# Encoder layer on one core: adaLN's second half behind the first tokens' turns, early gate weights in blocks of 256 columns, and the first gate pair's B22 product ahead of T1 and T4

## The chip, the core and the metric

The program runs on one core of one Trainium2 chip. Five engines work from queues of their own and meet only through semaphores: TensorE (PE, matrix products, with its weight loads shown as PEld), VectorE (DVE), ScalarE (ACT), GpSimd (POOL) and SyncE (SP, which here only issues DMA transfers). A queue is strictly in order: an instruction that waits holds up all that stands behind it. The metric is the time of one execution on the device in microseconds (us), the median of several runs; lower is better.

## What is computed

One layer of an encoder over 1280 tokens (1024 of a prompt and 256 of a sample) with 1024 channels, all in float32:

```python
mod = c @ w_ada + b_ada
shift, scale, gate = jnp.split(mod[:, None, :], 3, axis=-1)
h = rms_norm(x, norm_g) * (1.0 + scale) + shift
p = h @ w_in
cb, cc, cx, cz, q, k, v, o, mz, gpre, gmerge = split_combined(p)
...
g_conv, g_mlstm = jnp.split(jax.nn.sigmoid(gmerge), 2, axis=-1)
merged = g_conv * (y_conv @ w_proj_conv) + g_mlstm * (y_m @ w_proj_mlstm)
return x + gate * (merged @ w_out)
```

"adaLN" is the first line: the vector c (one for the prompt, one for the sample) times w_ada gives a shift and a scale for each channel. The change lies where h is made and where the first products with w_in begin, those of the 2048 merge-gate columns (gmerge).

## The kernel before

**Tiling.** h is held turned, channels on the partitions. It is cut in four blocks by channel half (1: channels 0 to 511, 2: 512 to 1023) and token half (1: tokens 0 to 639, 2: 640 to 1279): B11, B21 (second channels, first tokens), B12 (first channels, second tokens), B22. A pair of column blocks of w_in (128 columns each) against these four is done with seven products in place of eight (Strassen's scheme, class `Strassen`, lines 640 to 746): B11, B21, T2, T3, T1, T4 and B22, where T1 = B12 - B11, T2 = B22 - T1, T3 = T2 - B11 and T4 = B21 - T2 are sums of data blocks, and the weights of T2, T3, T1 and B22 are sums of weight blocks ("comb", made by VectorE in line 666). Each product has float32 precision by three terms: data and weights are both split in a rounded high part H and a rest L (ScalarE casts H in line 369, VectorE subtracts to get L in line 370; for weights ScalarE casts wh in line 317 and GpSimd subtracts to get wl in line 318), and wh·H + wh·L + wl·H are added up. One product is 24 matmuls of 128x320 (line 794): four slices of channels, and in each two with wh·H, two with wh·L, two with wl·H. Its result lies in one of three PSUM buffers ("acc") until VectorE adds it to what it belongs to (line 710).

**How the program begins** (`beginning`, from line 376). The ten token blocks of x are loaded and normalised, and turned by TensorE (`turn_x`, line 437); ScalarE (442) or VectorE (445) applies scale and shift as it takes the result out of PSUM. Scale and shift come from adaLN, eight loads of w_ada of 1 MB in two halves each (`load_wa`, `adaln(i)`, products in line 508): loads 0 to 3 give the values of channel half 1, loads 4 to 7 those of channel half 2. After the fourth and the eighth, VectorE copies the sum (515), TensorE turns it (519), and VectorE makes scale and shift (492 to 494). Tiles are shared: load 5 takes the place of load 2 (b10H), load 6 that of 3 (b10L), load 7 that of 4 (b11H), so each of them waits until the older one has been used.

**Early weights.** B11 and B21 are there before the others. So the B11 and B21 products of the first block of each of six gate pairs (class `Corner`) run first, six with B11 and six with B21; their weights come by `early_load(j, n)`, six loads of 512 KB, three for j = 0 (first channels) and three for j = 1. A loaded buffer ("raw") serves two corners. There are three such buffers in all. Then come the other five products of pair 0, of pair 1 and so on, from buffers of the same pool.

**The order of the work** is fixed when the program is built: `Board` (line 45 on) takes operations with assumed durations, the things that they read and write, and a due step, and lays them out per engine by a list plan, due steps first where more than one can begin at once. `op(..., after=...)` adds operations that must come before. On the chip the queues then run as laid out. Names for what follows: "pair 0" and "pair 1" are the first two gate pairs after the corners; their products run as T2, T3, T1, T4, B22 each.

Of the kernel before, what the change touches and what calls it, by code (L numbers as in the profile page):

```python
# [16 lines left out]
P = 128  # L17
# [23 lines left out]
class Board:  # L41
# [30 lines left out]
    def op(self, eng, us, f, r=(), w=(), after=(), low=False, slack=0.0):  # L72

        o = self.Op()
        o.eng, o.us, o.f, o.low, o.step, o.n, o.played, o.slack = eng, us, f, low, self.step, len(self.ops), False, slack
        o.before = set(after)
        for t in r:
            if t in self.writer:
                o.before.add(self.writer[t])
        for t in w:  # L80
            o.before.update(self.readers.get(t, ()))
            if t in self.writer:
                o.before.add(self.writer[t])
        for t in w:
            self.writer[t], self.readers[t] = o, []
        for t in r:
            if t not in w:
                self.readers.setdefault(t, []).append(o)
        o.before.discard(o)
        o.bufs = list(dict.fromkeys(b for t in (*r, *w) for b in (t if isinstance(t, tuple) else (t,)) if isinstance(b, self.Buf)))  # L90
        for b in o.bufs:
            b.users.append(o)
        self.ops.append(o)
        return o
# [87 lines left out]
def encoder_kernel(  # L182
# [7 lines left out]
    V, A, G, PE = nc.vector, nc.scalar, nc.gpsimd, nc.tensor  # L190
# [114 lines left out]
    def load(kb, dst, src, r, w, low=False):  # L305
        op("SP", kb, lambda: dma(dst(), src), r=r, w=w, low=low)
# [4 lines left out]
    def raw_tile():  # L311
        return buf(wp, [P, 4, 2 * P], F32, "raw", 3)
# [8 lines left out]
    raw_a = {}  # L321

    def early_load(j, n):

        raw_a[j, n] = raw_a[j, n + 2] = raw = raw_tile()
        for i in range(2):
            c = CGM + (n + 2 * i) * P
            load(256, lambda i=i: raw[:, :, i * P:(i + 1) * P], win[:, 4 * j:4 * j + 4, c:c + P], (), [(raw, i)])


    xt = {jl: [buf(xp, [P, TH2], F32, "xt", 17, xp.tile([P, TH2], F32, tag="xt", name="xt")) for _ in range(4)]
# [46 lines left out]
    def beginning():  # L378
# [48 lines left out]
        def turn_x(cs, kts):  # L427

            t0, tn = cs[0] * P, len(cs) * P
            l, smp = t0 // TH2, int(cs[0] > 7)  # L430
            for kt in kts:
                px = misc_buf()
                dst, d0 = xt[kt // 4, l][kt % 4], t0 % TH2

                def turn(px=px, kt=kt):
                    for j, c in enumerate(cs):
                        PE.transpose(px[:, j * P:(j + 1) * P], x_at[c][0]()[:, kt * P:(kt + 1) * P], ident[:])

                op("PE", .14 * len(cs), turn, r=[x_at[c][1] for c in cs], w=[px])
                sc, sh, tok = s1[:, kt, smp:smp + 1], shf[:, kt, smp:smp + 1], ("s1", kt // 4)  # L440
                if kt % 2 == (cs[0] in (3, 8)):
                    op("ACT", .37 + .1 * len(cs), lambda px=px, dst=dst, d0=d0, sc=sc, sh=sh: A.activation(
                        dst[:, d0:d0 + tn], px[:, :tn], AF.Identity, bias=sh, scale=sc), r=[px, tok], w=[(dst, int(d0 > 0))])
                else:
                    op("DVE", .39 + .1 * len(cs), lambda px=px, dst=dst, d0=d0, sc=sc, sh=sh: V.tensor_scalar(
                        out=dst[:, d0:d0 + tn], in0=px[:, :tn], scalar1=sc, scalar2=sh, op0=ALU.mult, op1=ALU.add),
                       r=[px, tok], w=[(dst, int(d0 > 0))])
# [8 lines left out]
        def later_rows(first):  # L456
# [22 lines left out]

            op("DVE", .5, take, r=[pr], w=["cwh"])  # L480
            op("POOL", .2, lambda: G.memset(ones[:], 1.0), r=[pr], w=[("rows", r) for r in (RSH, RNG, RMH, RCW, RCB)])
        pada = {}
        sel = const.tile([P, 2, 2], F32, name="sel")
        half = (lambda i: ident[:, 64 * i:64 * i + 64].rearrange("p (j r) -> p j r", r=32)[:, :, 0:2])
        op("DVE", .15, lambda: V.tensor_tensor(out=sel[:], in0=half(0), in1=half(1), op=ALU.add), w=["sel"])
# [10 lines left out]
        def adaln(i):  # L496

            hf = i // 4
            if i == 0:
                pada[0] = buf(psX, [P, 2, 512], F32, "acc", 3)  # L500
            t = pada[0]
            for n, (wa, tok) in enumerate(wa_at[i]):
                kt = 2 * (i % 4) + n

                def mm(n=n, kt=kt, wa=wa):
                    for j in range(2):
                        g = 32 * (2 * n + j)
                        PE.matmul(t[g:g + 32, hf, :], cz4()[:, kt, :], wa()[:, j * 512:(j + 1) * 512],
                                  start=i % 4 == 0, stop=i % 4 == 3, tile_position=(0, g))

                op("PE", 1.1, mm, r=[ctok, tok], w=[(t, hf)])
            if i % 4 < 3:
                return
            pm, m = misc_buf(), buf(cp, [P, 4, P], F32, "comb", 5)
            op("DVE", .65, lambda: V.tensor_copy(m[:].rearrange("p a b -> p (a b)"), t[:, hf, :]), r=[(t, hf)], w=[m])

            def turn_mod():
                for r in range(4):
                    PE.matmul(pm[:, 4 * r:4 * r + 4], m[:, r, :], sel[:].rearrange("p j s -> p (j s)"), start=True, stop=True)

            op("PE", .9, turn_mod, r=[m, "sel"], w=[pm])
            op("DVE", .6, lambda: modulation(hf, pm), r=[pm, "cols"], w=[("s1", hf)])
# [92 lines left out]
    class Slice:  # L615


        def __init__(self, b, sl):
            self.b, self.sl, self.tok = b, sl, (b, sl.start)
# [16 lines left out]
    class Strassen:  # L636

        def __init__(self, ca, cb, o11, o21, o12, o22, pre=None):  # L640
            self.cols, self.o, self.p1 = (ca, cb), (o11, o21, o12, o22), pre
            jobs = [(self.w_11, "b11", self.e_11), (self.w_12, "b21", self.e_12), (self.w_t2, "t2", self.e_t2),
                    (self.w_t3, "t3", self.e_t3), (self.w_t1, "t1", self.e_t1), (self.w_22, "t4", self.e_t4),
                    (self.w_b22, "b22", self.e_b22)]
            self.jobs, self.away = jobs if pre is None else jobs[2:], None

        def load(self):
# [90 lines left out]
        def e_t1(self, acc):  # L738
            self.out(3, acc, self.u3)
            self.plus(acc, self.u2, self.u2)  # L740

        def e_t4(self, acc):
            self.out(1, acc, self.u3, True)

# [12 lines left out]
    class Corner:  # L757
# [7 lines left out]
            self.st.e_11(acc)  # L765

        def prep(self, j):
            raw, i = raw_a[j, self.n], self.n // 2 % 2
            return split_op(lambda: raw[:, :, i * P:(i + 1) * P], [(raw, i)])

    todo, made, at = [], {}, [0]
# [42 lines left out]
            store(320, th_dr[r * P:(r + 1) * P, sl], t, [t.tok])  # L814
        return f

    def gate_pair(n, pre=None):

        return Strassen(CGM + n * P, CGM + (n + 1) * P,
                        (None, save(n, lo_)), (None, save(n + 1, lo_)),  # L820
                        (None, save(n, hi_)), (None, save(n + 1, hi_)), pre)

    def og_pair(n):

# [411 lines left out]
        store(256, ex_dr[i], lambda: place[:, 0:4 * P], [place])  # L1236


    sts = {n: gate_pair(n, max(n // 2 - 2, 0)) for n in range(0, 12, 2)}
    corners = {n: Corner(n, sts[n]) for n in sts}  # L1240
    for j in range(2):
        for n in (8, 10, 0, 2, 4, 6):
            add(corners[n], [j])
    for n in range(0, 16, 2):
        add(sts.get(n) or gate_pair(n))
    for st in head_pairs(range(1)):
        add(st)
    ends = [len(todo)]
# [655 lines left out]
```

## Time and profile before

| | |
|---|---|
| time, median of 3 runs | 1684.71 us (1683.56 to 1684.81) |
| the profiled execution | 1683.56 us, of which the span of its instructions 1681.4 us |
| TensorE busy | 1637.1 us, 97% of the span |
| VectorE, ScalarE, GpSimd busy | 59%, 34%, 40% |
| TensorE's waits of over 3 us in the first 130 us | 4.7 us (for c), 3.3 us (for a w_ada load), 3.5 us (for VectorE, line 370) |
| DMA | 240.82 MB, mean 143 GB/s; 351 GB/s in the first 42 us |

A line of a timeline gives start, duration, engine, line of the kernel, operation, destination and sources, and in brackets how long the engine was idle before it and what ended that. Rows of a stretch of the span ("windows") give its length, the busy time of each engine with the number of instructions, the granted TensorE clock (PEclk, 1.00 is full), the DMA engines' share and the rate. "T1" below is a product that reads tiles named xt, as T4 does; B22 reads b11H and b11L, T2 reads t2H and t2L, T3 reads t3H and t3L.

### The profile page before, as it was taken

To read this page: it belongs to the slowest core of one execution; us is meant where nothing else is said; L and a number is where in the kernel's file an instruction comes from. 1 tells how busy PE (TensorE), PEld (TensorE's weight loads), DVE (VectorE), ACT (ScalarE), POOL (GpSimd) and SP (SyncE) were. 2 spreads that over 40 slices of the span, in tenths; PEclk is the share of its full clock that TensorE was granted. 3 is DMA by queue.
4 is the path that set the end of the run, shared out by engine and by line. 5 is a ranking of instruction groups with operands and counts; after the bars stand their busy time and mean duration, and the time that the engine had idled before them with its cause. 6 is when DMAs were issued, how large, how long until landed. Compare 5 with 4: busy or idle time off the path is not lost.

```text
span 1681.4 us, 27662 instructions
## 1 busy us (share of the span) xinstructions
PE 1637.1 (97%) x10528; PEld 1563.3 (93%) x10528; DVE 992.3 (59%) x1691; ACT 573.3 (34%) x1115; POOL 680.2 (40%) x499
## 2 busy tenths in 40 slices
PE   6999999999999999999999999999999999899997
PEld 2999999999999999999999999999888899898985
DVE  5785334555555566566666876651257677555655
ACT  3643332134553222222222212212256665333322
POOL 1233333335664666667666633333210102323412
PEclk8999999999999999999999999999999999999999
DMA  9334335324553122222122556458778855773631
GB/s 351 111 126 133 103 99 123 77 72 124 144 154 103 51 71 69 82 82 70 54 66 82 143 132 141 118 132 278 258 242 293 270 180 170 237 266 107 245 105 63
DMA packets 281528, 240.82 MB, mean 143 GB/s; under 512 B 96068, under 2 KB 236596, under 8 KB 281396
## 3 DMA queue, kind: packets, MB, share of 16 engines
q1 hardware_dynamic: 281364, 239.05, 47.1%
q8 instruction: 83, 1.36, 0.3%
q14 instruction: 49, 0.40, 0.1%
q10 hardware_dynamic: 32, 0.01, 0.0%
HBM read 170.12 MB, written 68.89 MB: 142 GB/s over the span
## 4 chain that ended last, share of the span: by engine, by line
PE 91%; DMA 4%; DVE 3%; ACT 1%; SPq 1%; issue 1%; DVEq 0%; ACTq 0%
PE acc L794 63%; PE u L1423 3%; PE qc L1383 3%; PE accd L1578 2%; PE accd L1579 2%; PE accd L1580 2%; PE accd L1792 2%; PE accd L1791 2%; PE accd L1790 2%; PE acc L1646 2%; PE acc L1647 2%; PE acc L1645 2%; PE misc L1506 1%; DMA b11H<-in_w_ada_dram 1%; PE misc L1466 1%; DVE xt L375 1%
## 5 line engine op out<-in xcount | busy, mean ns | idle before, releaser
L318 POOL TENSOR_TENSOR wl<-comb,wh 128x512 fp32r<-128x512 f32 x176 | 249.9, 1420 | 288.2 <-ACT wh L317 279.5
L710 DVE TENSOR_TENSOR q<-acc,q 128x640 f32<-128x640 f32 x272 | 220.9, 819 | 222.1 <-PE acc L794 219.8
L318 POOL TENSOR_TENSOR wl<-raw,wh 128x512 fp32r<-128x512 f32 x136 | 190.2, 1399 | 225.0 <-ACT wh L317 208.1
L794 PE MATMUL acc<-xt,wh 128*128 128x320 f32 x1408 | 265.3, 310 | 3.5 <-DVE xt L370 3.5
L794 PEld LDWEIGHTS acc<-xt,wh 128*128 128x128 f32 x1408 | 221.9, 189 | 4.0 <-DVE xt L370 3.8
L317 ACT CAST wh<-comb 128x512 fp32r<-128x512 f32 x176 | 108.8, 619 | 292.7 <-PE acc L794 268.8
L317 ACT CAST wh<-raw 128x512 fp32r<-128x512 f32 x136 | 84.3, 620 | 271.3 <-PE acc L794 213.2
L794 PE MATMUL acc<-xt,wl 128*128 128x320 f32 x704 | 161.0, 310 | 0.0
L1606 POOL TENSOR_TENSOR wl<-raw,wh 128x512 fp32r<-128x512 f32 x28 | 36.7, 1313 | 225.5 <-ACT wh L1605 219.2
L794 PEld LDWEIGHTS acc<-xt,wl 128*128 128x128 f32 x704 | 118.2, 189 | 0.0
L666 DVE TENSOR_TENSOR comb<-raw 128x512 f32<-128x512 f32 x88 | 71.7, 815 | 40.1 <-POOL wl L318 18.6
L861 POOL TENSOR_TENSOR big<-big,q 128x640 f32<-128x640 f32 x48 | 78.3, 1631 | 35.9 <-DVE q L710 27.6
L610 ACT ACTIVATE q<-q,zero 128x640 f32<-128x640 f32 x76 | 63.1, 831 | 82.9 <-DVE q L710 77.3
L666 DVE TENSOR_TENSOR comb<-raw,comb 128x512 f32<-128x512 f32 x44 | 46.7, 1062 | 63.0 <-POOL wl L318 62.9
L794 PE MATMUL acc<-b00H,wh 128*128 128x320 f32 x352 | 81.8, 314 | 0.0
L794 PE MATMUL acc<-b10H,wh 128*128 128x320 f32 x352 | 80.4, 310 | 0.8 <-ACT q L724 0.8
L794 PE MATMUL acc<-b11H,wh 128*128 128x320 f32 x352 | 81.1, 312 | 0.0
L1578 PE MATMUL accd<-y,wh 128*128 128x320 f32 x256 | 80.0, 313 | 0.8 <-DVE og L1556 0.8
L794 PE MATMUL acc<-b00L,wh 128*128 128x320 f32 x352 | 80.2, 309 | 0.1
L794 PE MATMUL acc<-t3H,wh 128*128 128x320 f32 x352 | 80.3, 309 | 0.0
L794 PE MATMUL acc<-t2L,wh 128*128 128x320 f32 x352 | 80.3, 309 | 0.0
L794 PE MATMUL acc<-t2H,wh 128*128 128x320 f32 x352 | 80.3, 309 | 0.0
(316 smaller groups left out, 4112.8 us busy)
## 6 DMA issues: line engine op xcount, KB each, us to landing
raw<-in_w_in_dram SPq DMA_DIRECT2D x108, 256.0 KB
raw<-in_w_in_dram SPq DMA_DIRECT2D x40, 512.0 KB
th<-th_dr SPq DMA_DIRECT2D x32, 320.0 KB
th_dr<-q SPq DMA_DIRECT2D x28, 320.0 KB
raw<-in_w_proj_conv_dram SPq DMA_DIRECT2D x16, 512.0 KB
raw<-in_w_proj_mlstm_dram SPq DMA_DIRECT2D x16, 512.0 KB
raw<-in_w_out_dram SPq DMA_DIRECT2D x16, 512.0 KB
k<-kn_dr SPq DMA_DIRECT2D x56, 128.0 KB
```

What stands on the lines that cost most here:

```text
L317: op("ACT", .63, lambda: A.copy(wh[:], src()), r=r, w=[wh])
L318: op("POOL", 1.4, lambda: G.tensor_tensor(out=wl[:], in0=src(), in1=fp(wh[:]), op=ALU.subtract), r=[*r, wh], w=[wl])
L610: A.activation(out, in_, AF.Tanh, bias=zero[:, 0:1], scale=0.5)
L666: op("DVE", .9, lambda: V.tensor_tensor(out=t[:], in0=x(), in1=y(), op=o), r=[x.tok, y.tok], w=[t])
L710: op("DVE", .82, lambda: V.tensor_tensor(out=two(dst()), in0=acc[:, :, 0:TQ], in1=two(t()), op=ALU.add), r=[acc, t.tok], w=[dst.tok])
L794: PE.matmul(acc[:, q, 0:TQ], st_[:, k_, :], m_[:, q * TQ:(q + 1) * TQ], start=k_ == 0 and n == 0, stop=k_ == 3 and n == 2)
L861: op("POOL", 1.65, lambda: G.tensor_tensor(out=dst(), in0=dst(), in1=t(), op=ALU.mult), r=[dst.tok, t.tok], w=[dst.tok])
L1383: PE.matmul(pq[:, 0:HD + 2], qTs[i][:, kd, c * P:(c + 1) * P], C[:, kd, :], start=kd == 0, stop=kd == 1)
L1423: PE.matmul(pu[:, db, 0:HD + 2], k[:, db * P:(db + 1) * P], wv[:], start=True, stop=True)
L1578: PE.matmul(accs[q][:, :TQ], wh, yH, start=kt == 0, stop=False)
L1579: PE.matmul(accs[q][:, :TQ], wh, yL, start=False, stop=False)
L1606: op("POOL", 1.36, lambda wh=wh, wl=wl, src=src: G.tensor_tensor(out=wl[:], in0=src(), in1=fp(wh[:]), op=ALU.subtract), r=[raw, wh], w=[wl])
```

## The change

Three edits.

1. `turned` collects the operations of `turn_x`. adaLN's product of load 4 (the first of the second half) gets the last turn noted so far as an operation that must come before it: the last turn of the first 640 tokens in channel half 1.
2. An early load takes 256 neighbouring columns in one transfer, in place of two blocks of 128 columns that lie 256 columns apart in two transfers. For that the first six gate pairs are no longer (0,1), (2,3) and so on but (0,2), (1,3), (4,6), (5,7), (8,10), (9,11). Their own loads, which were one transfer of 256 columns for each channel half, become two of 128 columns.
3. The first pair gets `late=True`: its products run as T2, T3, B22, T1, T4 in place of T2, T3, T1, T4, B22, with the sums that its results go through rearranged to fit (`e_b22_first`, `e_t1_last`; the number of additions is the same).

```diff
     def early_load(j, n):
-        raw_a[j, n] = raw_a[j, n + 2] = raw = raw_tile()
-        for i in range(2):
-            c = CGM + (n + 2 * i) * P
-            load(256, lambda i=i: raw[:, :, i * P:(i + 1) * P], win[:, 4 * j:4 * j + 4, c:c + P], (), [(raw, i)])
+        raw_a[j, n] = raw_a[j, n + 1] = raw = raw_tile()
+        c = CGM + n * P
+        load(512, lambda: raw[:], win[:, 4 * j:4 * j + 4, c:c + 2 * P], (), [(raw, 0), (raw, 1)])
...
-                op("PE", .14 * len(cs), turn, r=[x_at[c][1] for c in cs], w=[px])
+                turned.append(op("PE", .14 * len(cs), turn, r=[x_at[c][1] for c in cs], w=[px]))
...
-                op("PE", 1.1, mm, r=[ctok, tok], w=[(t, hf)])
+                op("PE", 1.1, mm, r=[ctok, tok], w=[(t, hf)], after=turned[-1:] if i == 4 else ())
...
-        def __init__(self, ca, cb, o11, o21, o12, o22, pre=None):
+        def __init__(self, ca, cb, o11, o21, o12, o22, pre=None, late=False):
...
+            if late:
+                jobs = [*jobs[:4], (self.w_b22, "b22", self.e_b22_first), (self.w_t1, "t1", self.e_t1_last), jobs[5]]
...
+        def e_b22_first(self, acc):
+            self.plus(acc, self.u2, self.u2)
+
+        def e_t1_last(self, acc):
+            self.out(3, acc, self.u3)
+            self.out(2, acc, self.u2, True)
...
-            raw, i = raw_a[j, self.n], self.n // 2 % 2
+            raw, i = raw_a[j, self.n], self.n % 2
...
-    def gate_pair(n, pre=None):
+    def gate_pair(n, m, pre=None, late=False):
...
-    sts = {n: gate_pair(n, max(n // 2 - 2, 0)) for n in range(0, 12, 2)}
+    sts = {n: gate_pair(n, n + 2, max(i - 2, 0), i == 0) for i, n in enumerate((0, 1, 4, 5, 8, 9))}
     corners = {n: Corner(n, sts[n]) for n in sts}
     for j in range(2):
-        for n in (8, 10, 0, 2, 4, 6):
+        for n in (8, 9, 0, 1, 4, 5):
             add(corners[n], [j])
-    for n in range(0, 16, 2):
-        add(sts.get(n) or gate_pair(n))
+    for n in (0, 1, 4, 5, 8, 9, 12, 14):
+        add(sts.get(n) or gate_pair(n, n + 1))
```

What the plan makes of it is seen best at two places. In the changed program the line numbers of these functions are lower by one up to line 634, and products stand in line 802 in place of 794, comb in 667, evictions in 711.

**SyncE's queue around adaLN's last load.** The last w_ada load is the second row with b11H; raw are early weights, p_dr a store of a corner. Before:

```order
L306 DMA b10L<-in_w_ada_dram 128x2x512 x2
L306 DMA raw<-in_w_in_dram 128x4x128 x2
L306 DMA b11H<-in_w_ada_dram 128x2x512 x2
L306 DMA raw<-in_w_in_dram 128x4x128 x2
L309 DMA p_dr<-q 128x640
```

With the change:

```order
L306 DMA b10L<-in_w_ada_dram 128x2x512 x2
L306 DMA raw<-in_w_in_dram 128x4x256 x2
L306 DMA b11H<-in_w_ada_dram 128x2x512 x2
L309 DMA p_dr<-q 128x640
L306 DMA ones<-in_mh_norm_g_dram 8x128
```

One more early weight load (512 KB) now stands ahead of the last w_ada load: five in all in place of four. On TensorE, in the same stretch, the products of load 4 move from between the turns to behind the last of them. Before, from the turn of the first half's result on:

```order
L519 MATMUL misc<-sel,comb 128x4 x4
L437 MATMUL misc<-ident,t3H 128x128 x2
L437 MATMUL misc<-ident,t3L 128x128
L508 MATMUL acc<-b11H,big 32x512 x2
L437 MATMUL misc<-ident,t3L 128x128
L437 MATMUL misc<-ident,b11L 128x128
L437 MATMUL misc<-ident,t3H 128x128 x2
```

With the change, the piece with the last turn of the first tokens and all that adaLN's loads 4, 5 and 6 need:

```order
L436 MATMUL misc<-ident,t3L 128x128
L436 MATMUL misc<-ident,b11L 128x128
L507 MATMUL acc<-b11H,big 32x512 x4
L507 MATMUL acc<-b10H,big 32x512 x4
L507 MATMUL acc<-b10L,big 32x512 x4
```

Load 7's products follow three product slices later, in both programs right ahead of the last product slice before the second half's turn (519); up to there both have done the same seven product slices.

**After T3 of pair 0.** TensorE before:

```order
L794 MATMUL acc<-t3H,wh 128x320 x2
L794 MATMUL acc<-t3L,wh 128x320 x2
L794 MATMUL acc<-t3H,wl 128x320 x2
L794 MATMUL acc<-xt,wh 128x320 x4
L794 MATMUL acc<-xt,wl 128x320 x2
```

With the change:

```order
L802 MATMUL acc<-t3H,wh 128x320 x2
L802 MATMUL acc<-t3L,wh 128x320 x2
L802 MATMUL acc<-t3H,wl 128x320 x2
L802 MATMUL acc<-b11H,wh 128x320 x2
L802 MATMUL acc<-b11L,wh 128x320 x2
```

B22 follows T3, where T1 did. VectorE at the same place, from the sums of T4's data (the first row) and the L parts of T1 (second row) on, before:

```order
L375 TENSOR_TENSOR xt<-xt 128x640 x4
L370 TENSOR_TENSOR xt<-xt 128x640 x4
L710 TENSOR_TENSOR q<-acc,big 128x640
L370 TENSOR_TENSOR xt<-xt 128x640 x4
L710 TENSOR_TENSOR q<-acc,q 128x640
L710 TENSOR_TENSOR big<-acc,big 128x640
L710 TENSOR_TENSOR q<-acc,q 128x640
L666 TENSOR_TENSOR comb<-raw 128x512
L666 TENSOR_TENSOR comb<-raw,comb 128x512
```

With the change:

```order
L374 TENSOR_TENSOR xt<-xt 128x640 x4
L369 TENSOR_TENSOR xt<-xt 128x640 x4
L711 TENSOR_TENSOR q<-acc,big 128x640
L369 TENSOR_TENSOR xt<-xt 128x640 x4
L711 TENSOR_TENSOR big<-acc,big 128x640
L711 TENSOR_TENSOR q<-acc,q 128x640
L711 TENSOR_TENSOR big<-acc,big 128x640
L711 TENSOR_TENSOR q<-acc,q 128x640
L667 TENSOR_TENSOR comb<-raw 128x512
L667 TENSOR_TENSOR comb<-raw,comb 128x512
```

The two combs at the end, T3's and B22's weights of pair 1, now stand behind four evictions (B22, T1 twice, T4) in place of three (T1 twice, T4).

More of the change, by code (lines that the diff above doesn't have):

```diff
@@ L481, in later_rows @@
             op("POOL", .2, lambda: G.memset(ones[:], 1.0), r=[pr], w=[("rows", r) for r in (RSH, RNG, RMH, RCW, RCB)])
-        pada = {}
+        pada, turned = {}, []
         sel = const.tile([P, 2, 2], F32, name="sel")
@@ L815, in save @@
         return f
-    def gate_pair(n, pre=None):
-        return Strassen(CGM + n * P, CGM + (n + 1) * P,
-                        (None, save(n, lo_)), (None, save(n + 1, lo_)),
-                        (None, save(n, hi_)), (None, save(n + 1, hi_)), pre)
+    def gate_pair(n, m, pre=None, late=False):
+        return Strassen(CGM + n * P, CGM + m * P,
+                        (None, save(n, lo_)), (None, save(m, lo_)),
+                        (None, save(n, hi_)), (None, save(m, hi_)), pre, late)
     def og_pair(n):
```

## The prediction

> **What bounds the kernel now.** I read the page first.
>
> ```profile
> span 1681.4 us, 27662 instructions
> PE 1637.1 (97%) x10528; PEld 1563.3 (93%) x10528; DVE 992.3 (59%) x1691; ACT 573.3 (34%) x1115; POOL 680.2 (40%) x499
> ```
>
> TensorE bounds the span; it idles for 44 us in all. The change adds and removes no matmul, so it can only win idle time or time at a low granted clock, and only where it acts. The second view is TensorE's list of waits in the first 130 us.
>
> ```profile
> PE acc L794 <- DVE xt L370: 3.5, 1, 3.5
> PE acc L508 <- DMA b11H<-in_w_ada_dram: 2.0, 2, 1.7
> ```
>
> Two things matter: w_ada loads (line 508) and one wait for the L part of T1. The chain of waits says which of them ends last.
>
> ```profile
> 38.14 8.55 DMA b11H<-in_w_ada_dram
> 46.73 1.05 PE acc L508 x4
> ```
>
> Up to 46.7 us the last w_ada load (load 7) sets the time. From there TensorE works without a gap to 99.6 us, while VectorE runs a row of sums that is late at T1; TensorE's timeline there:
>
> ```profile
> 99.60 0.46 PE L794 MATMUL acc<-xt,wh 128*128 128x320 f32 x2
> 103.59 0.56 PE L794 MATMUL acc<-xt,wh 128*128 128x320 f32 x2 [3.54 <-DVE xt L370]
> ...
> 108.46 0.75 PE L794 MATMUL acc<-xt,wh 128*128 128x320 f32 x4
> ...
> 111.98 0.31 PE L794 MATMUL acc<-b11H,wh 128*128 128x320 f32 x1
> ```
>
> T4 runs from 108.46 to 111.98: a product is 3.52 us, a slice 0.88, two matmuls 0.29 (rounded up; four are 0.59). T1 issues two matmuls at 99.60 and stands from 99.89 to 103.59: 3.70 us lost. Its other 3.23 us of work then take 4.87 (to 108.46), 1.64 more than they should. The windows show why:
>
> ```profile
> 100.00:104.40 4.40, 0.86 (x6) 0.81 (x6) 4.40 (x6) 2.27 (x4) 1.86 (x1) 1.00 0.14 54
> 104.40:107.80 3.40, 3.40 (x15) 3.40 (x14) 3.29 (x5) 0.72 (x1) 0.00 (x0) 0.50 0.00 0
> 107.80:111.20 3.40, 3.40 (x25) 3.40 (x24) 3.19 (x5) 0.43 (x1) 0.00 (x0) 1.00 0.00 0
> ```
>
> After the wait the granted clock is 0.50 for 3.4 us; a stretch full of work ends it. So T1's place costs 3.70 + 1.64 = **5.34 us**. Behind it nothing is lost for long:
>
> ```profile
> 124.00:290.00 166.00, 166.00 (x1134) 166.00 (x1133) 71.39 (x91) 50.16 (x73) 60.75 (x47) 1.00 0.41 116
> ```
>
> So what is won by then stays won to the end, since TensorE stays the bound.
>
> **Edit 3, B22 ahead of T1 and T4.** VectorE's order of work is nearly the same, so I take its times from its timeline, and ScalarE's and GpSimd's behind it:
>
> ```profile
> 102.73 3.02 DVE L370 TENSOR_TENSOR xt<-xt 128x640 fp32r<-128x640 f32 x4
> 105.67 0.81 DVE L710 TENSOR_TENSOR q<-acc,big 128x640 f32<-128x640 f32 x1
> 106.40 3.60 DVE L370 TENSOR_TENSOR xt<-xt 128x640 fp32r<-128x640 f32 x4
> 109.92 0.82 DVE L710 TENSOR_TENSOR q<-acc,q 128x640 f32<-128x640 f32 x1
> 110.65 0.81 DVE L710 TENSOR_TENSOR big<-acc,big 128x640 f32<-128x640 f32 x1
> 112.18 0.82 DVE L710 TENSOR_TENSOR q<-acc,q 128x640 f32<-128x640 f32 x1 [0.71 <-PE acc L794]
> 114.45 2.55 POOL L318 TENSOR_TENSOR wl<-comb,wh 128x512 fp32r<-128x512 f32 x2 [12.33 <-ACT wh L317]
> 116.96 1.30 POOL L318 TENSOR_TENSOR wl<-raw,wh 128x512 fp32r<-128x512 f32 x1
> ```
>
> Step by step, with VectorE's times unchanged:
> - B22 runs from 99.60 to 103.12 (its data have been ready since before T2). T1 issues two matmuls to 103.41, gets its first L at 103.59 as now, and ends at 106.82 (3.23 later, at the full clock, since no long wait comes before). Lost: 0.18.
> - T4: four L parts in 3.60 us, the last ready at 110.00, a little slower than the 0.88 of a slice; behind the last one come 0.04 of signal and four matmuls, so T4 ends at 110.63. Lost: 0.29.
> - T2 of pair 1 needs B22's PSUM buffer. That eviction stands behind T4's L parts and takes 109.92 to 110.74; T2 runs from 110.78 to 114.30. Lost: 0.15.
> - T3 of pair 1 is where the stall goes. Its weights wait behind four evictions on VectorE: 0.73 apart, they begin at 109.92, 110.65, 111.38 and 112.11. In the trace the weights' L (wl) was ready 3.57 us after the last eviction before the comb began (112.18 to 114.45 + 1.30): comb, tanh and cast on ScalarE, subtraction on GpSimd. Now that is 112.11 + 3.57 = 115.68. T3 does its first four matmuls to 114.89 and stands to 115.72. Lost: 0.83. It ends 2.93 later, at 118.65.
>
> Before, the product behind it began at 122.54:
>
> ```profile
> 122.54 0.75 PE L794 MATMUL acc<-xt,wh 128*128 128x320 f32 x4
> ```
>
> So the edit wins 3.89 us: 5.34 less the new 1.45. The cover for the rest is GpSimd, which needs 1.30 us for a weight block where TensorE needs 3.52; the next blocks are in time.
>
> This all hangs on VectorE's row of sums. If that runs later by s, everything from T1's first L on does, and the gain is 3.89 - s. Edits 1 and 2 set s.
>
> **Edit 2, the loads.** Before load 7 the change puts five early loads of 0.524 MB in place of four, but with runs of 1 KB in place of 512 B. Rates while the queues are full, from windows in which only one kind moves (first 512 B, then two with 1 KB, then 2 and 4 KB):
>
> ```profile
> 21.00:23.00 2.00, 1.36 (x6) 0.14 (x4) 1.55 (x6) 0.47 (x1) 0.00 (x0) 1.00 1.23 292
> 83.00:84.00 1.00, 1.00 (x9) 1.00 (x8) 1.00 (x3) 0.96 (x2) 0.84 (x1) 1.00 1.00 352
> 83.00:85.00 2.00, 2.00 (x16) 2.00 (x15) 2.00 (x6) 1.56 (x2) 0.84 (x1) 1.00 1.00 334
> 29.00:31.00 2.00, 2.00 (x8) 0.55 (x6) 1.74 (x3) 0.72 (x1) 0.00 (x0) 0.50 1.02 408
> ```
>
> Four loads at 292 GB/s are 7.18 us, five at 343 (between 352 and 334) are 7.64: load 7 lands 0.46 later; I take 0.4. Bounds: at 408 it is 0.75 earlier; if 1 KB were no better than 512 B (292), 1.80 later. The Trainium skill (DMA: Bandwidth & Descriptors, section Specifications) gives 512 B as the least transfer for line rate; by that rule runs of 512 B lose nothing, the 1.80 holds, and the sum would be 1682.8. The rows above speak against it.
>
> The other side of the edit: pair 1's own loads become four transfers with 512 B in place of two. VectorE waits for just these, and goes on without a gap from there to 110 us:
>
> ```profile
> 87.73 0.69 DVE L666 TENSOR_TENSOR comb<-raw 128x512 f32<-128x512 f32 x1 [0.97 <-DMA raw<-in_w_in_dram]
> ```
>
> 1.05 MB at 292 are 3.59 us, at 352 2.98: 0.6 more at most. At least 0, since a lone 512 KB moves alike in both forms (512 B, then 1 KB):
>
> ```profile
> 54.20:56.20 2.00, 2.00 (x17) 1.96 (x16) 1.86 (x3) 0.87 (x3) 0.00 (x0) 1.00 0.88 248
> 65.20:67.20 2.00, 2.00 (x17) 1.94 (x16) 1.23 (x2) 1.87 (x4) 0.00 (x0) 1.00 0.86 256
> ```
>
> I take 0.2, nearer to the lone pair, because these four are issued over more than a microsecond. It passes through to T1 in full. Later pairs' loads have several microseconds of room, and the next stage loads in the same halves at full TensorE work; cost 0.
>
> **Edit 1, adaLN's second half.** TensorE's order up to load 7's products holds the same work, and it waits for loads there, so moving load 4's products costs and wins nothing by itself. What it moves is when load 7 may be issued, since that overwrites load 4's tile:
>
> ```profile
> 35.32 3.35 SPq L306 DMA_DIRECT2D b11H<-in_w_ada_dram  x2
> 37.66 0.33 PE L437 MATMUL misc<-ident,t3L 128*128 128x128 f32 x1
> 42.23 1.05 PE L508 MATMUL acc<-b10L,big 128*32 128x512 f32 x4 [0.99 <-DMA b10L<-in_w_ada_dram]
> 45.36 1.05 PE L508 MATMUL acc<-b11H,big 128*32 128x512 f32 x4
> ```
>
> The last turn stood at 37.66 with 3.8 us of load 4's products ahead of it; without them I estimate 34 to 36, then 2.1 us of products (eight matmuls; 1.05 for four) or 3.8 at the slow clock: done at 36 to 40. SyncE finished issuing load 7 at 38.67, and 8.55 us passed from there to its landing, all of it backlog of other loads. So an issue up to about 4 us later is hidden. Behind SyncE's waiting row stand only a corner's store and small copies. Load 6 lands earlier (three early loads ahead of it: 0.8 us), so the three slices now between loads 6 and 7 (load 6's second products at 42.23 - 0.8, then 1.05 and 2.64: 45.1) end before load 7's first half, 45.36 + 0.4. Cost 0.
>
> **Sum.** s = 0.4 + 0.2 = 0.6; gain 3.89 - 0.6 = 3.3 us. Against the profiled execution (1683.56: span 1681.44 and 2.1 around it) this is 1680.3; it ran 1.15 below the median of 1684.71, so the forecast is **1681.4** in median. s lies between -0.75 and 2.4, the gain between 1.5 and 4.6.
>
> **Rivals.**
> - *Loads faster*: 1 KB runs reach 408 GB/s and pair 1's loads cost nothing. Gain 4.6: 1680.1. For: 2 KB runs do it; against: the 334 window.
> - *Loads late*: s = 2.4, gain 1.5: 1683.2. The edit then only trades T1's wait for a later start. For: a fifth load ahead of load 7 is sure; against: 352.
> - *Slower: the clock stays low through adaLN.* In place the turns now run with no products between:
>
> ```profile
> 25.90:29.30 3.40, 2.72 (x8) 1.06 (x9) 0.51 (x3) 0.67 (x1) 2.71 (x3) 0.50 1.04 407
> 29.30:32.70 3.40, 3.40 (x12) 1.18 (x10) 3.30 (x6) 1.15 (x2) 0.00 (x0) 0.50 1.03 410
> ```
>
> Already now the clock is 0.50 here, with load 4's products in both stretches. The chain has what they take then:
>
> ```profile
> 26.58 1.92 PE acc L508 x4
> ```
>
> If it stayed so to load 7, loads 4 to 7 would take 1.92 us a half in place of 1.05 and the three slices 5.3: from 35, 4 x 3.84 + 5.3 ends at 55.7 in place of 47.8. s is then 8.1 and the time 1684.71 + 4.2 = 1688.9. It decides only from 3.9 us of delay on, and the first full stretch (104.4 to 107.8) ended the low clock before; I give it little. The Trainium skill (TensorE: Matmul & The Clock Gate, Part 4: PE-mode transpose) says transposes do not count as busy in the same way; by that rule the low clock lasts until the first slices and adaLN products, one stretch more, which load 7 still hides. The sum stays.
> - *The change does not do what it says*: T1 again meets an L that is not there. It needs s of over 3.5, so it belongs to the last case.
>
> **Chances.** Forecast 0.60, loads faster 0.17, loads late 0.18, slower 0.05. A change of 0.2% (3.37 us) is about what a measurement here tells from none, and the forecast's 3.3 lies on it: I count 0.28 of its 0.60 as faster, 0.32 as within. With the fast case faster is 0.45, with the late loads the same is 0.50, slower 0.05. Range: 1679.4 to 1684.9 takes in both load cases and some of the run-to-run spread (1.25); the likeliest's own is 1680.4 to 1682.6.
>
> **What would show it.** Right: no wait over 1 us at T1 and no 0.50 clock near 104; a wait of about 0.8 in T3 of pair 1 for GpSimd's wl; load 7's second products near 47.1; VectorE's wait for raw near 88, about 1 us; T1 of pair 1 beginning near 119.3. Wrong: load 7 beyond 48; a long wait for PSUM behind VectorE's four evictions; a low clock after 40.

## The result and the profile after

The change takes 1680.42 us in median of 9 runs (1678.55 to 1681.34), the kernel before 1684.71 in 9 runs beside it: ratio 0.9972, 95% interval 0.9963 to 0.9981, 4.3 us faster. In a second comparison it was 1680.33 against 1684.69: 0.9976 (0.9967 to 0.9985). The forecast was 1681.4 with a range of 1679.4 to 1684.9; the time lies in the range, 1.0 below the forecast. The gain of 0.28% (0.24% the second time) is just past the 0.2% that the prediction counted as the bound between faster and the same, to which it gave 0.45 and 0.50. The profiled execution took 1680.06, its span is 1678.2.

The page's first part: TensorE is busy 1.9 us longer than before, and its idle time falls by 5.1 us (44.3 to 39.2); the span is shorter by the difference.

```profile
PE 1639.0 (98%) x10528; PEld 1566.4 (93%) x10528; DVE 993.8 (59%) x1691; ACT 572.9 (34%) x1115; POOL 679.9 (41%) x499
```

The chain of waits around 47 us (start, duration, what): load 7 still ends it. It came 46.73 before, so it is 0.32 later.

```profile
37.24 9.77 DMA b11H<-in_w_ada_dram
...
47.05 1.05 PE acc L507 x4
```

TensorE's timeline from the end of B22 on (T1, T4, T2, T3 and T1 of pair 1):

```profile
103.43 0.92 PE L802 MATMUL acc<-xt,wh 128*128 128x320 f32 x4
...
107.12 0.90 PE L802 MATMUL acc<-xt,wh 128*128 128x320 f32 x4
...
110.99 0.56 PE L802 MATMUL acc<-t2H,wh 128*128 128x320 f32 x2
...
114.61 0.50 PE L802 MATMUL acc<-t3H,wh 128*128 128x320 f32 x2
...
115.92 0.56 PE L802 MATMUL acc<-t3H,wl 128*128 128x320 f32 x2 [0.52 <-POOL wl L318]
...
118.95 0.75 PE L802 MATMUL acc<-xt,wh 128*128 128x320 f32 x4
```

There is no wait at T1. The only one of TensorE's between 48 and 290 us that lasts over 0.2 us is the 0.52 in T3 of pair 1, for GpSimd's wl. T1 of pair 1 begins 3.59 us earlier than before (122.54).

VectorE's row of sums, which the prediction took over with a delay s:

```profile
87.81 0.69 DVE L667 TENSOR_TENSOR comb<-raw 128x512 f32<-128x512 f32 x1 [0.79 <-DMA raw<-in_w_in_dram]
...
102.92 3.02 DVE L369 TENSOR_TENSOR xt<-xt 128x640 fp32r<-128x640 f32 x4
...
106.60 3.60 DVE L369 TENSOR_TENSOR xt<-xt 128x640 fp32r<-128x640 f32 x4
110.12 0.82 DVE L711 TENSOR_TENSOR big<-acc,big 128x640 f32<-128x640 f32 x1
...
113.04 0.69 DVE L667 TENSOR_TENSOR comb<-raw 128x512 f32<-128x512 f32 x1
```

All of it is 0.19 to 0.20 later than before (102.73, 106.40). And the clock in the stretch that was at 0.50 before (length, busy time of PE, PEld, DVE, ACT, POOL, granted clock, DMA share, GB/s):

```profile
104.40:107.80 3.40, 3.40 (x24) 3.25 (x23) 3.29 (x6) 0.82 (x2) 0.00 (x0) 1.00 0.00 0
```

### The profile page after: what moved, and what is told of

It reads as the page before. It is cut to its first block, busy times and chain, and to the rows that moved or that the text cites. A ratio compares the mean times of both kernels' runs of the same rounds, so it can differ in the third digit from the quotient of the medians.

```text
span 1678.2 us, 27669 instructions
## 1 busy us (share of the span) xinstructions
PE 1639.0 (98%) x10528; PEld 1566.4 (93%) x10528; DVE 993.8 (59%) x1691; ACT 572.9 (34%) x1115; POOL 679.9 (41%) x499
## 4 chain that ended last, share of the span: by engine, by line
PE 94%; DMA 2%; DVE 2%; ACT 1%; issue 1%; SPq 0%; POOL 0%; DVEq 0%; ACTq 0%; POOLq 0%
PE acc L802 65%; PE u L1431 3%; PE qc L1391 3%; PE accd L1586 2%; PE accd L1587 2%; PE accd L1588 2%; PE accd L1800 2%; PE accd L1799 2%; PE accd L1798 2%; PE acc L1654 2%; PE acc L1653 2%; PE acc L1655 2%; PE misc L1514 1%; PE misc L1474 1%; PE misc L436 1%; DMA b11H<-in_w_ada_dram 1%
## 5 line engine op out<-in xcount | busy, mean ns | idle before, releaser
L802 PE MATMUL acc<-t3H,wl 128*128 128x320 f32 x352 | 80.3, 309 | 0.5 <-POOL wl L318 0.5
L802 PE MATMUL acc<-b00H,wl 128*128 128x320 f32 x352 | 80.4, 310 | 0.0
```

The costliest lines, as they stand in the source:

```text
L802: PE.matmul(acc[:, q, 0:TQ], st_[:, k_, :], m_[:, q * TQ:(q + 1) * TQ], start=k_ == 0 and n == 0, stop=k_ == 3 and n == 2)
```

## The experiments

What was open after the result: is the gain edit 3's alone, what do edits 1 and 2 cost or bring each, and is the wait that is left worth anything. All runs are below; "load 7" is the start of load 7's second products, "T1 of pair 1" the start of that product in the profiled execution. Medians stand beside those of the kernel before on the same chip. Interval is the 95% interval of the ratio.

| kernel | load 7 | T1 of pair 1 | median, before | ratio, interval |
|---|---|---|---|---|
| before | 46.73 | 122.54 | 1684.71 | |
| the change (edits 1, 2, 3) | 47.05 | 118.95 | 1680.42, 1684.71 | 0.9972 (0.9963 to 0.9981) |
| edit 3 | 46.65 | 118.55 | 1680.67, 1684.42 | 0.9978 (0.9969 to 0.9988) |
| edits 1, 2 | 47.14 | 123.84 | 1684.72, 1684.42 | 1.0000 (0.9991 to 1.0009) |
| edits 2, 3 | 45.59 | 117.47 | 1679.09, 1684.42 | 0.9966 (0.9954 to 0.9979) |
| edits 1, 3 | 48.33 | 120.22 | 1682.35, 1684.42 | 0.9988 (0.9979 to 0.9997) |
| edits 2, 3, earlier comb | 46.61 | 117.72 | 1678.93, 1684.79 | 0.9958 (0.9946 to 0.9971) |
| the same, load 7 first | 42.61 | 115.78 | 1675.86, 1684.79 | 0.9944 (0.9930 to 0.9957) |
| the change, load 7 first | 41.60 (both halves) | 116.99 | 1675.55, 1684.79 | 0.9948 (0.9933 to 0.9964) |
| the change, L 1.5 us late | 46.95 | 120.62 | 1682.03, 1684.79 | 0.9983 (0.9974 to 0.9992) |
| edit 1 | 48.71 | 124.42 | 1686.72, 1684.69 | 1.0010 (1.0001 to 1.0019) |
| the change again | 46.50 (both halves) | 119.17 | 1680.33, 1684.69 | 0.9976 (0.9967 to 0.9985) |
| edits 2, 3, earlier comb, load 7 first, again | 42.70 | 115.87 | 1676.19, 1684.69 | 0.9950 (0.9936 to 0.9963) |

**Edit 3 alone.** The kernel before, with the first pair's order and sums of the change:

```diff
-    sts = {n: gate_pair(n, max(n // 2 - 2, 0)) for n in range(0, 12, 2)}
+    sts = {n: gate_pair(n, max(n // 2 - 2, 0), n == 0) for n in range(0, 12, 2)}
```

> Edit 3 alone on the kernel before: B22 ahead of T1 and T4 in pair 0, adaLN and all loads as before. Theory (the gain is T1's stall and its low clock, less four small waits; the loads only shift it): load 7's second products at 46.7 as before, no wait over 0.5 us at T1, a wait of 0.5 to 0.8 in T3 of pair 1, T1 of pair 1 at 118.6 to 118.8, about 0.2 earlier than the change's 118.95; time 3.6 to 3.9 us below before, some 0.2 to 0.3 better than the change. Rival (the gain comes from the loads, edits 1 and 2): within 1 us of before.

TensorE's timeline:

```profile
46.65 1.05 PE L508 MATMUL acc<-b11H,big 128*32 128x512 f32 x4 [0.36 <-DMA b11H<-in_w_ada_dram]
...
115.52 0.56 PE L803 MATMUL acc<-t3H,wl 128*128 128x320 f32 x2 [0.51 <-POOL wl L318]
...
118.55 0.75 PE L803 MATMUL acc<-xt,wh 128*128 128x320 f32 x4
```

T1 of pair 1 is 3.99 us earlier than before and 0.40 earlier than in the change; the median is 3.75 below before. The theory holds, and by T1 of pair 1 edits 1 and 2 together do not add to the gain but take a little from it; the medians (3.75 and 4.3) can't tell so little.

**Edits 1 and 2 without edit 3.**

```diff
-    sts = {n: gate_pair(n, n + 2, max(i - 2, 0), i == 0) for i, n in enumerate((0, 1, 4, 5, 8, 9))}
+    sts = {n: gate_pair(n, n + 2, max(i - 2, 0)) for i, n in enumerate((0, 1, 4, 5, 8, 9))}
```

> The change without edit 3: edits 1 and 2 alone. Theory: load 7's second products near 47.05 as in the change, the row of sums on VectorE 0.2 later than before, T1 waits 3.7 us again and the clock is 0.50 for 3.4 us behind it; T1 of pair 1 near 122.7, time 0.2 us above before (between 0 and +0.5). Rival (the loads bring the gain): 3 to 4 us below before.

T1 in TensorE's timeline, then the windows behind it:

```profile
103.87 0.90 PE L802 MATMUL acc<-xt,wh 128*128 128x320 f32 x2 [3.40 <-DVE xt L369]
...
123.84 0.75 PE L802 MATMUL acc<-xt,wh 128*128 128x320 f32 x4
```

```profile
102.80:106.22 3.42, 2.35 (x9) 2.35 (x10) 3.42 (x6) 1.45 (x2) 0.00 (x0) 0.50 0.00 0
106.22:109.63 3.41, 3.41 (x15) 3.41 (x15) 3.10 (x5) 0.00 (x0) 0.00 (x0) 0.51 0.00 0
```

The wait is back, and the low clock with it, here for two stretches in place of one, so T1 of pair 1 came 1.1 later than expected (123.84, not 122.7). The median is within 0.3 of before: without edit 3 there is no gain, as the theory had it.

**Edit 1 alone.**

```diff
-                op("PE", 1.1, mm, r=[ctok, tok], w=[(t, hf)])
+                op("PE", 1.1, mm, r=[ctok, tok], w=[(t, hf)], after=turned[-1:] if i == 4 else ())
```

> Edit 1 alone on the kernel before: load 4's products behind the last turn of the first tokens, which also moves load 7 behind a fifth early load (512 B runs). Theory (edit 1 costs one early load in load 7's landing): load 7's second products at 48.3 to 48.5 (one load of 0.524 MB at 292 GB/s is 1.8 later than 46.7), T1's wait of 3.5 and the low clock stay, time 1.5 to 1.9 above before. Rival (the prediction's: edit 1 costs nothing): load 7 at 46.7, time as before.

```profile
48.71 1.05 PE L508 MATMUL acc<-b11H,big 128*32 128x512 f32 x4 [0.27 <-DMA b11H<-in_w_ada_dram]
...
105.46 0.83 PE L794 MATMUL acc<-xt,wh 128*128 128x320 f32 x2 [3.44 <-DVE xt L370]
...
124.42 0.75 PE L794 MATMUL acc<-xt,wh 128*128 128x320 f32 x4
```

Load 7 lands 1.98 us later, T1 of pair 1 begins 1.88 later, the median is 2.0 above before. So edit 1, which the prediction had at no cost, costs near 2 us by itself. How: load 7 overwrites load 4's tile. With load 4's products behind all turns, the plan has load 7 wait longer and puts the early load that stood behind it ahead of it. SyncE's queue with edit 1 alone:

```order
L306 DMA b10L<-in_w_ada_dram 128x2x512 x2
L306 DMA raw<-in_w_in_dram 128x4x128 x4
L306 DMA b11H<-in_w_ada_dram 128x2x512 x2
L309 DMA p_dr<-q 128x640
```

The four raw rows are two early loads; before, one of them stood behind load 7. The fifth early load that the prediction put down to edit 2 is edit 1's.

**Edits 1 and 3, without the blocks of 256 columns.** Edit 2's lines are undone:

```diff
-        raw_a[j, n] = raw_a[j, n + 1] = raw = raw_tile()
-        c = CGM + n * P
-        load(512, lambda: raw[:], win[:, 4 * j:4 * j + 4, c:c + 2 * P], (), [(raw, 0), (raw, 1)])
+        raw_a[j, n] = raw_a[j, n + 2] = raw = raw_tile()
+        for i in range(2):
+            c = CGM + (n + 2 * i) * P
+            load(256, lambda i=i: raw[:, :, i * P:(i + 1) * P], win[:, 4 * j:4 * j + 4, c:c + P], (), [(raw, i)])
```

> The change without edit 2: edits 1 and 3, early loads in two transfers with runs of 512 B. The plan keeps five early loads ahead of load 7, so only the length of the runs differs from the change. Theory (512 B runs move at 292 GB/s, 1 KB runs at 343, while the queues are full): 1.3 us more for five loads of 0.524 MB, load 7's second products at 48.2 to 48.5, the row of sums on VectorE 1.2 later, T1 of pair 1 near 120.2, time about 1.2 us slower than the change. Rival (512 B is enough for the full rate, as the Trainium skill, DMA: Bandwidth & Descriptors, section Specifications, has it): load 7 at 47.05, time as the change.

```profile
48.33 1.05 PE L508 MATMUL acc<-b11H,big 128*32 128x512 f32 x4 [0.23 <-DMA b11H<-in_w_ada_dram]
...
120.22 0.75 PE L803 MATMUL acc<-xt,wh 128*128 128x320 f32 x4
```

Load 7 is 1.28 us later than in the change, T1 of pair 1 1.27: the 1.3 that the two rates, 292 and 343 GB/s, give for five loads. The median is 1.9 above the change's. So runs of 1 KB are worth 1.3 us here, and the rule of the Trainium skill (DMA: Bandwidth & Descriptors, section Specifications), that 512 B is enough for the full rate, does not hold here with the queues full. One thing goes along with the runs: without edit 2 the same bytes go in transfers of 256 KB in place of 512 KB, and no run tells the two apart.

**Edits 2 and 3 without edit 1.**

```diff
-                op("PE", 1.1, mm, r=[ctok, tok], w=[(t, hf)], after=turned[-1:] if i == 4 else ())
+                op("PE", 1.1, mm, r=[ctok, tok], w=[(t, hf)])
```

> The change without edit 1: edits 2 and 3. The plan then puts load 4's products between the turns again, and load 7's first half behind four early loads, its second half behind five. Theory (edit 1 costs and wins nothing): load 7's second products within 0.4 of 47.05, time within 0.5 us of the change, with the low clock of the turns ending earlier than the change's 33.6 to no use. Rival (edit 1 lets load 7 be issued in time): load 7's second products at 48 or later and 1 us or more slower than the change.

SyncE's rows for load 7 and the early load between its halves, then its products:

```profile
31.24 0.55 SPq L306 DMA_DIRECT2D b11H<-in_w_ada_dram  x1
32.50 0.45 SPq L306 DMA_DIRECT2D raw<-in_w_in_dram  x1
33.83 1.77 SPq L306 DMA_DIRECT2D b11H<-in_w_ada_dram  x1
```

```profile
42.64 1.05 PE L507 MATMUL acc<-b11H,big 128*32 128x512 f32 x4 [0.34 <-DMA b11H<-in_w_ada_dram]
...
45.59 1.05 PE L507 MATMUL acc<-b11H,big 128*32 128x512 f32 x4
...
117.47 0.75 PE L802 MATMUL acc<-xt,wh 128*128 128x320 f32 x4
```

Three early loads stand ahead of these rows (two issued at 14.97, one at 24.68). So load 7's first half has three ahead of it and its second half four, not four and five as expected; in the change both have five. The first half is used 3.1 us earlier than in the change (45.75), as two loads of 0.524 MB at 343 GB/s would have it, the second 1.46 earlier. T1 of pair 1 begins 1.48 us earlier. Neither theory is right: edit 1 is not free, and leaving it out is a gain. In times: 5.3 below before, where the change is 4.3 and 4.4; the intervals overlap, so the 1.5 rests on the traces and on edit 1 alone.

**Edits 2 and 3 with an earlier comb.**

```diff
-            board.step = k - (8 if k < 18 else 2)
+            board.step = 14.5 if k == 18 else k - (8 if k < 18 else 2)
```

> Edits 2 and 3 without edit 1 (as in the run without turns), and the comb for T3's weights of pair 1 due at step 14.5 in place of 16: on VectorE it now stands behind B22's eviction and ahead of T1's two. Theory (the remaining wait in T3 of pair 1 comes only from the comb's place behind four evictions): that wait of 0.5 is gone, T1 of pair 1 begins at 116.9 to 117.0 in place of 117.47, time 0.5 us below the run without turns, about 5.8 below before. Rival (the evictions pushed back by 0.7 us hold up a PSUM buffer that T3 needs): a wait for VectorE of 0.3 to 0.7 in its place, time as the run without turns.

```profile
46.61 1.05 PE L507 MATMUL acc<-b11H,big 128*32 128x512 f32 x4
...
117.72 0.75 PE L802 MATMUL acc<-xt,wh 128*128 128x320 f32 x4
```

TensorE has no wait at all between 48 and 130 us, so the rival falls. T1 of pair 1 begins 71.11 us behind load 7's second products, where it was 71.88 without the comb's move: 0.77 won. The expected 117.0 was missed since load 7's products themselves came 1.0 later in this execution, behind a stretch of low clock (40.74 to 44.15, shown below). In the medians (1678.93, and 1679.09 without the move) the 0.8 can't be told from nothing.

**Load 7 first.** The early loads are held until load 7 has been issued, in the last kernel and in the change:

```diff
-        load(512, lambda: raw[:], win[:, 4 * j:4 * j + 4, c:c + 2 * P], (), [(raw, 0), (raw, 1)])
+        load(512, lambda: raw[:], win[:, 4 * j:4 * j + 4, c:c + 2 * P], (), [(raw, 0), (raw, 1)],
+             after=last_wa)
...
+                if i == 7:
+                    last_wa.append(o)
```

> The kernel of the run with the earlier comb, and load 7 ahead of the early loads (0,4) and (1,8), which it followed wholly or with its second half; (1,0) stays behind it. The plan now puts load 7's products right behind load 6's, and four product slices that stood before them come after. Both theories: load 7's second products at about 42.5 in place of 45.6, since 1.05 MB less is ahead of it at 343 GB/s. Theory 1 (as the prediction reckoned: all behind follows load 7 one for one): T1 of pair 1 at about 113.9, time 3 us better. Theory 2 (work that TensorE had done while it waited counts as much): four slices of 0.88 are given back, T1 of pair 1 near 117.4, time within 0.7 us of the run with the earlier comb.

> The change with load 7 ahead of the three early loads (0,4), (1,8) and (1,0). Edit 1 stays, so load 7 is still issued only after load 4's products behind the turns, near 37. Theory (edit 1 costs 1.5 us by load 7's place behind one more early load, and its later issue is hidden as long as the queues are full): load 7's second products near 42.5 to 43.5; three product slices (2.64) move behind it, T1 of pair 1 at 117.0 to 118.0. Rival (the late issue sets the landing): the DMA queues run empty before load 7, its second products at 44.5 or later, T1 of pair 1 at 119 or later.

Without edit 1, and with the earlier comb:

```profile
40.60 1.05 PE L512 MATMUL acc<-b11H,big 128*32 128x512 f32 x4 [0.27 <-DMA b11H<-in_w_ada_dram]
42.61 1.05 PE L512 MATMUL acc<-b11H,big 128*32 128x512 f32 x4 [0.96 <-DMA b11H<-in_w_ada_dram]
...
115.78 0.75 PE L807 MATMUL acc<-xt,wh 128*128 128x320 f32 x4
```

Load 7's second products begin where both theories had them (42.5). T1 of pair 1 lies between the theories, at 115.78: load 7 came 4.0 earlier than in the kernel it was made from, T1 of pair 1 1.94. So what TensorE had done while it waited does count, but not in full. A count of the slices takes the difference apart: from load 7's second products to T1 of pair 1 TensorE does 73 product slices where it did 70, so three were given back (2.64 us) and not the four that were expected. And from the start of T1 to T1 of pair 1 it takes 14.09 in place of 14.69, T1 and T4 now at full pace (slices of 0.88 throughout), probably since the slices put behind load 7 give VectorE time. 4.00 - 2.64 + 0.60 = 1.96.

The change with load 7 first; SyncE's row, then TensorE's:

```profile
36.48 0.88 SPq L306 DMA_DIRECT2D b11H<-in_w_ada_dram  x2
```

```profile
41.60 3.29 PE L512 MATMUL acc<-b11H,big 128*32 128x512 f32 x8 [0.30 <-DMA b11H<-in_w_ada_dram]
...
116.99 0.75 PE L807 MATMUL acc<-xt,wh 128*128 128x320 f32 x4
```

Load 7 is issued as late as in the change (36.78 there) and yet its products begin 4.15 us earlier (45.75). So the late issue is hidden, as the prediction had it; what edit 1 costs is the place behind one more early load. T1 of pair 1 is 1.96 earlier than in the change. The median, 1675.55, is of four runs that lie between 1673.92 and 1680.77, and can't be told from the 1675.86 of the kernel without edit 1.

**T1's L parts 1.5 us late.** Two more operations of the same form, into the tile that the first L part then overwrites:

```diff
+                lo, x = MOV["t1"][1][0], B12[0]
+                for _ in range(2):
+                    op("DVE", .83, lambda: V.tensor_tensor(out=lo(), in0=x[:], in1=x[:], op=ALU.subtract),
+                       r=[(x, 0), (x, 1)], w=[MOV_B["t1"][1][0]])
```

> The change with the first L part of T1 worked out three times on VectorE, so that all L parts of T1 and T4 come 1.5 us later (two more operations of 0.755). Same result. Theory (what is late on VectorE passes to TensorE one for one, and a wait of 1.7 us is too short to bring the low clock): T1 waits 1.7 us, clock 1.00 behind it, T1 of pair 1 at 120.4 to 120.5, time 1.5 us slower than the change. Rival (any wait over 1 us brings the 0.50 clock back for 3.4 us): T1 of pair 1 at 121.6 to 122.2 and 3 us slower than the change.

```profile
105.44 0.56 PE L806 MATMUL acc<-xt,wh 128*128 128x320 f32 x2 [1.64 <-DVE xt L369]
...
120.62 0.75 PE L806 MATMUL acc<-xt,wh 128*128 128x320 f32 x4
```

T1 waits 1.64, T1 of pair 1 begins 1.67 later than in the change, and the median is 1.6 above the change's. The clock stays at 1.00. Lateness of VectorE passes on one for one; a wait of this length costs itself alone, one of 3.4 or more (edits 1 and 2, edit 1 alone, before) costs the low clock as well.

**Once more, side by side.** The change as it is, and the kernel without edit 1, with the earlier comb and load 7 first:

> The change once more, beside the other two on the same chip. All theories: 4 to 4.5 us below before, 2.3 to 2.9 below edit 3 with edit 1 undone is not to be seen here; against edit 1 alone about 6 lower, against load 7 first 4 to 5 higher.

> Edits 2 and 3 with load 7 ahead of three early loads and the earlier comb, once more beside the change. Theory (T1 of pair 1 begins 3.2 us earlier than in the change, 6.8 earlier than before, and TensorE works without a gap from load 7 to 288 us; what more there is in the times comes from low-clock stretches after 1150 us that fall otherwise): 6.5 to 9 us below before, 3 to 4.5 below the change. Rival (the first time was a lucky draw of later stages): within 1 us of the change.

1680.33 and 1676.19, with 1684.69 for before. (One clause of the first expectation is garbled; its figures are those against before, 4.4 measured, against edit 1 alone, 6.4, and against load 7 first, 4.1.) The second is 8.5 us below before (8.9 the first time) and 4.1 below the change, so it beats both kernels, in both comparisons. T1 of pair 1 begins at 115.87 there, 6.7 before the kernel before, and this lead is still 6.7 at 1150 us. The other 2 us of the median are not seen in a trace: the profiled execution, the slowest of its five, ends only 5.2 before the other. As far as the traces tell, they come from behind 1150 us (last section).

## Why the prediction was right, and where it was not

- **What bounds the kernel, and the price of T1's place.** Right. In the four kernels with B22 first, the comb in its old place and the early loads not held back (edit 3; edits 1, 3; edits 2, 3; the change), T1 of pair 1 begins 71.9 us behind load 7's second products; before it was 75.81 (122.54 - 46.73). The difference is 3.91; the prediction's edit 3 was worth 3.89.
- **Edit 3's four new losses.** The starts quoted above give them, each product being 3.52 without loss: T1 3.69, T4 3.87, T2 3.62, T3 of pair 1 4.34. That is 0.17, 0.35, 0.10 and 0.82, 1.44 in sum; predicted were 0.18, 0.29, 0.15 and 0.83, 1.45. The wait shown in T3 is shorter than the loss (0.52 against 0.82), since the shown duration of a group of matmuls reaches past the start of the next; losses are read from start to start.
- **s.** Predicted 0.6, from 0.4 for load 7 and 0.2 for pair 1's own loads. Load 7 was 0.32 later. Pair 1's loads cost nothing that shows: VectorE's wait for raw fell from 0.97 to 0.79. On VectorE's row of sums, where the prediction defines s, it was 0.20. s is the term that made the forecast too small at this place: 3.59 won at T1 of pair 1 in place of 3.3 (3.37 in the second profile of the change). By the prediction's own rule that would have won 3.89 - 0.20 = 3.69; where the other 0.10 went was not taken apart.
- **Whose 0.32 it is.** This step failed. "Edit 1 ... Cost 0" and "Edit 2 ... load 7 lands later; I take 0.4" split the sum wrongly: the prediction counted the fifth early load under edit 2. Measured at T1 of pair 1, edit 1 costs 1.88 alone, 1.67 beside edit 3 and 1.48 beside edits 2 and 3; edit 2 wins 1.27 beside edits 1 and 3 and 1.08 beside edit 3. The sum came out all the same, and not by luck: the prediction priced the queue as it was built, five loads with runs of 1 KB against four with 512 B. What it had wrong is which edit does what, and so it missed that leaving edit 1 out would be better. The parts of edit 1's reasoning that were tested held: the last turn was at 35.4, load 4's products were done at 36.8, the three slices ended at 45.2, and a late issue is hidden. (One reading there was off: the 8.55 us to load 7's landing count from 38.14, not from the end of its issue at 38.67, so 8.0 passed from there; nothing hangs on it.) What was overlooked is that the plan, not the chip, answers the later use of the tile, with another order of SyncE's queue.
- **The rate of the loads.** Right: 1.3 us for five loads from 292 and 343 GB/s, 1.28 measured. The rival "loads late" falls, and so does, for these loads, the rule of the Trainium skill (DMA: Bandwidth & Descriptors, section Specifications) that stands beside it in the prediction; "loads faster" did not happen either (load 7 did not come earlier), though the time came near that case.
- **The slower rival.** The clock was low in one piece from 20.4 to 34.0 us in the first profile of the change, which load 7 hid. In the second it was low in shorter pieces, one of them from 40.5 to 43.9: the "low clock after 40" that the prediction named as a sign against itself. It cost little, for load 7 was still to come: T1 of pair 1 began at 119.17 in place of 118.95.

```profile
23.40:26.80 3.40, 2.85 (x13) 2.48 (x13) 2.37 (x5) 1.80 (x4) 3.40 (x3) 0.50 1.06 392
...
33.60:37.00 3.40, 3.40 (x24) 2.30 (x25) 3.23 (x11) 2.28 (x4) 0.00 (x0) 0.94 1.05 380
```

- **"What is won then stays won to the end."** Right up to 1150 us, where the lead on the kernel before is unchanged (the product on xt that begins at 1149.69 there begins at 1146.11, 3.58 earlier); behind that not quite: in the first profile of the change the span is 3.20 shorter, where 3.59 was won. The median's 4.3 is more than either. The late stage varies by about this much from execution to execution, so the agreement of the time to 1 us says less than that of the places.

## What to carry to other kernels

When a planner sets the order, build each edit alone and look at the queues that it gives before costing it: two edits costed together here had 1.5 to 1.9 us of cost and 1.1 to 1.3 of gain, and only the sum looked harmless. Where loads bound a stage, what counts for a load is what stands ahead of it in the queue and how long its runs are, and not when it is issued as long as the queues are full; so ask of every moved use of a tile which load it lets in ahead. And price a wait by the distance between two marks on both sides of it (load 7 to T1 of pair 1), which stays the same to 0.1 us over four kernels whose medians differ by up to 3.

## What the runs showed of the hardware that was not expected

The clock falls without a long wait. The trace has the granted clock in stretches of 3.41 us; cut along them, the busy time of TensorE in one stretch goes with the clock of the next. Windows of before, at T1, and twice in the late stage (the stretch ahead of a fall, and two that are followed by 1.00):

```profile
100.99:104.40 3.41, 0.81 (x5) 0.81 (x6) 3.41 (x5) 1.46 (x2) 1.13 (x1) 1.00 0.00 0
...
1169.36:1172.78 3.42, 1.82 (x12) 1.85 (x13) 0.89 (x2) 0.62 (x1) 1.84 (x2) 1.00 1.08 357
1438.99:1442.42 3.43, 1.69 (x12) 1.43 (x10) 1.73 (x7) 2.74 (x7) 1.90 (x2) 1.00 0.27 64
1442.42:1445.84 3.42, 1.32 (x7) 0.89 (x8) 2.92 (x5) 0.91 (x2) 0.65 (x1) 1.00 0.92 277
1445.84:1449.25 3.41, 3.41 (x15) 3.41 (x14) 0.63 (x1) 0.72 (x1) 0.00 (x0) 0.50 0.96 322
```

The change with load 7 first, and the kernel with the earlier comb:

```profile
38.01:41.42 3.41, 1.50 (x8) 0.14 (x4) 2.50 (x6) 0.72 (x1) 0.00 (x0) 1.00 1.02 333
41.42:44.83 3.41, 3.23 (x9) 0.39 (x9) 0.62 (x1) 0.00 (x0) 0.00 (x0) 0.50 1.07 360
```

```profile
37.33:40.74 3.41, 1.32 (x8) 0.29 (x8) 2.96 (x9) 0.19 (x1) 0.00 (x0) 1.00 1.05 381
40.74:44.15 3.41, 3.41 (x12) 0.38 (x8) 0.83 (x1) 0.54 (x1) 0.00 (x0) 0.50 1.07 365
```

And the change with late L parts, where the clock stayed:

```profile
103.09:106.50 3.41, 1.77 (x12) 1.51 (x12) 3.34 (x5) 0.73 (x1) 0.00 (x0) 1.00 0.00 1
106.50:109.92 3.42, 3.42 (x24) 3.27 (x23) 3.32 (x5) 0.73 (x1) 0.00 (x0) 1.00 0.00 0
```

In these rows stretches with 0.81 to 1.50 us of work are followed by 0.50, those with 1.69 to 1.82 by 1.00, and in the kernel with the earlier comb the longest wait of such a stretch was 1.8 us. All thirteen traces, cut alike from 13 us on, put the limit at about 1.6 us, near half a stretch: a stretch at full clock with less than 1.58 was always followed by 0.50, and one with more than 1.60 by 1.00, except among the turns. There, in stretches that begin between 20 and 25 us, the shown work was up to 2.32 us and the clock fell all the same, as with edits 2 and 3:

```profile
21.09:24.50 3.41, 2.31 (x15) 1.15 (x14) 2.60 (x6) 1.14 (x2) 0.65 (x1) 1.00 1.09 361
24.50:27.91 3.41, 2.63 (x9) 0.57 (x8) 0.71 (x3) 1.71 (x3) 3.41 (x4) 0.50 1.05 402
```

By the limit of 1.6 the 1.64 us wait of the late L parts, in a stretch with 1.77 us of work, was spared by 0.2 us of work or so. Turns and the small matmuls between them seem to count for less than their shown time; how much was not measured. The Trainium skill (TensorE: Matmul & The Clock Gate, Part 1) names one idle window of about 3.4 us as what throttles; the length of the window agrees, but it need not be idle.

This can account for part of the scatter of total times. Where stretches of the late stage are half full, it depends on where the 3.41 us grid falls. In the first profile of the change, one had 1.25 us of work, and the next was at half clock:

```profile
1163.82:1167.24 3.42, 1.25 (x9) 0.99 (x7) 0.33 (x1) 1.24 (x2) 2.13 (x2) 1.00 1.07 367
1167.24:1170.65 3.41, 3.10 (x12) 3.13 (x13) 0.56 (x2) 0.00 (x0) 0.40 (x1) 0.50 1.09 360
```

The second profile of the same kernel has no such fall there. The four runs of the change with load 7 first go the same way: spans of 1672.1 and 1672.3 us at a mean granted clock of 0.995, 1675.2 at 0.992, 1679.0 at 0.991. Whether a shift of the work by 3 us moves these falls on the average, and so whether any of the 2 us by which the medians of the kernel with edits 2 and 3, the earlier comb and load 7 first exceed its lead at T1 of pair 1 is more than chance, stays open: it was not tried.
